# A hybrid attention layer on one core: the framework schedules by its other model of engine times, and the fillers' matmuls are pinned in source order

## The chip, the core and the metric

The kernel runs on one core of a Trainium2 chip. A core has TensorE (PE, matmuls, with its weight loads shown apart as PEld), VectorE (DVE), ScalarE (ACT), GpSimd (POOL) and SyncE (SP, which here issues the DMAs). Each engine works through a program of its own in order, and semaphores make one wait for another. The metric is the time of one execution on the device in microseconds (us).

## The reference

One layer of a hybrid encoder on 1024 positions of width 1024, in float32: a combined input projection, two attention branches of eight heads each with a head dimension of 64, sigmoid gates, an output projection, LayerNorm, a SwiGLU feed-forward part (FFN) and a second LayerNorm.

```python
h = x @ w_in[l]
qa, ka, va, qb, kb, vb, ga, gb = jnp.split(h, split_pts, axis=-1)
y_a = chunk_band_attention(heads_a(qa), heads_a(ka), heads_a(va), rel_bias[l]) @ w_proj_a[l]
y_b = stick_breaking_attention(heads_b(qb), heads_b(kb), heads_b(vb)) @ w_proj_b[l]
gate_a = jax.nn.sigmoid(ga + b_gate[l, :D])
gate_b = jax.nn.sigmoid(gb + b_gate[l, D:])
mix = (gate_a * y_a + gate_b * y_b) @ w_out[l]
x = layer_norm(DEEPNORM_ALPHA * x + mix, ln1_g[l], ln1_b[l])
g, u = jnp.split(x @ w_ffn_in[l], 2, axis=-1)
x = layer_norm(DEEPNORM_ALPHA * x + (jax.nn.silu(g) * u) @ w_ffn_out[l], ln2_g[l], ln2_b[l])
```

Branch A is a softmax over a band of nine chunks of 64 keys with a learned bias. Branch B (stick-breaking) weighs each key by the sigmoid of its score times the product of one minus the sigmoids of the keys between it and the query.

## The kernel before

**Arithmetic.** Every float32 operand of a large product is split into a high and a low part (`split`, L110: a cast on ACT, then a subtraction on DVE), and one product becomes three matmuls, high by high, high by low and low by high. The names end in h and l: wbp1h and wbp1l are the halves of one weight operand of pair 1.

**Stages, in the order of the source.**
- *Projection.* The first pair of weight tiles is multiplied plainly (`project_plain`); each further pair goes through a scheme of seven products for two by two blocks (`pair_steps`, L181). It accumulates in banks of the matmul memory that are named sx, sy and sz, copies them out on ACT and adds them on DVE (L191, tiles c). The operands for it are sums of blocks of x (s13, s24) and of the weights (ta, tb, with wa and wb as their split forms, wc for the last product), which DVE works out (L153 to L157, L277 to L280).
- *Attention.* Heads a0 to a7 of branch A, then b0 to b7 of branch B, each in two groups of four blocks of 128 queries. A block of A (`soft_block`) is: scores on PE (sc_a, L506 and L507), a reduction with bias on DVE (L539), an exponential on ACT, a reciprocal on DVE and a multiplication on POOL (L547). A block of B (`stick_block`) is: scores, two sigmoids on ACT (L572, L573), a running product on DVE (L574) and a product on POOL (L577). Then `value_steps` transposes the weights on PE (tp, L603), splits them (pt) and multiplies them with the values (pv, L617 and L618); a copy on ACT (L627) and an addition on DVE (L631) make the head's result.
- *Fillers.* Between the steps of attention, the generator `fill_all` hands out single matmuls of other work: gate projections (gps, L463) and, from the middle of branch B, the output projection of branch A (yAps, L665).
- *After attention.* The last head pair's result is split into yh7 and yl7, then come the projection of branch B (yBps, matmuls in `mm3`, L118 to L121), the product with w_out (ops), the first LayerNorm, transposes of its result (x1ps, L865), the FFN's up projection in the scheme of seven products (sxf, syf, szf, and plainf for the tile without a partner), its down projection (dn) and the second LayerNorm.

**What sets the order.** The source traces instructions in one order: the loop over the attention's steps runs blocks ahead by the table LEAD, transposes, and takes fillers until the amount given by FILL is used. The framework then schedules: it goes through the program with a model of engine times, and on each engine puts next the first instruction in source order whose inputs are ready by that model. So an instruction traced later can be put ahead of one traced earlier. Tiles share slots and banks in turn (BANKS: two each for mm and sc, three for tr, one for pv), and a new owner waits for the readers of the old one. The result is one fixed list for each engine.

Names in listings below: sc_a3_4_0 is the score bank of head 3 of A, block 4, first part; w_a3_0_2 the weights of head a3, group 0, block 2; tp_a3_0_0 the transposed weights of a group's first pack; the numbers at the end of a name are running numbers of tiles.

## Time and profile before

| | us |
|---|---|
| median of 3 runs | 1448.25 |
| the three runs | 1447.61, 1448.25, 1448.53 |
| the profiled execution's own time | 1447.76 |
| its span in the trace | 1446.0 |

The profile is of one execution. In its rows of groups, "x96 | 100.6, 1057 | 49.5 <-DVE" reads: 96 instructions, 100.6 us in total, 1057 ns each in the mean, 49.5 us of idle time of the engine just ahead of them, most of it ended by DVE. In a timeline each row is the start, the duration, the engine and the line; a value in brackets is the idle time before, and what ended it. PE's matmuls are pipelined, so their durations overlap, and its pace is read from start to start. Line numbers are those of the kernel before; in the changed kernel all lines from 86 on are higher by one.

### The profile page before, as it was taken

Reading aid. Unit: us, or ns where it says so; the run is one execution under the profiler, and the core shown is the slowest. Engines: PE = TensorE matmul, PEld = TensorE weight load, DVE = VectorE, ACT = ScalarE, POOL = GpSimd, SP = SyncE. Lnnn points to the kernel's source line nnn. Section 1 sums busy time; section 2 is a strip of 40 time slices with the busy share of each in tenths; the row PEclk is TensorE's granted clock in tenths of the full one; section 3 lists DMA queues with packets and bytes.
Section 4 is the critical chain, followed back from the end, with each engine's and each line's share of the span. In section 5 each row is a group of like instructions: output and inputs, shape, how many; then the busy total and the mean of one; then the engine's idle time right before and its main releaser. Section 6 shows DMA issues by size and latency. Waiting matters only on the chain.

```text
span 1446.0 us, 18952 instructions
## 1 busy us (share of the span) xinstructions
PE 1411.3 (98%) x6656; PEld 1163.9 (80%) x6656; DVE 1022.1 (71%) x1591; ACT 687.3 (48%) x1204; POOL 313.3 (22%) x339
## 2 busy tenths in 40 slices
PE   7999999999999999999999999999999999999997
PEld 6788888888888788788887878888888788888886
DVE  7867676744888888787769995555565544885996
ACT  6445444435777879784323543333333332444540
POOL 0000000003434769652304021111111101300012
PEclk9999999999999999999999999999999999999999
DMA  6566686748656466757861233233222226863521
GB/s 233 172 216 223 216 266 201 294 155 235 189 166 185 137 192 193 218 171 279 315 234 73 81 138 107 105 109 110 95 90 93 95 102 241 305 210 111 174 80 73
DMA packets 84238, 248.75 MB, mean 172 GB/s; under 512 B 10400, under 2 KB 10400, under 8 KB 84144
## 3 DMA queue, kind: packets, MB, share of 16 engines
q1 hardware_dynamic: 84144, 247.56, 51.7%
q8 instruction: 52, 0.85, 0.3%
q14 instruction: 42, 0.34, 0.1%
HBM read 164.39 MB, written 83.13 MB: 171 GB/s over the span
## 4 chain that ended last, share of the span: by engine, by line
PE 84%; DVE 8%; ACT 3%; DMA 2%; issue 2%; POOL 1%; SPq 0%; POOLq 0%; DVEq 0%; ACTq 0%
PE dn L1145 14%; PE sxf L178 14%; PE sxp L178 12%; PE szf L178 6%; PE szp L178 6%; PE ops L1004 5%; PE gps L463 4%; PE syf L178 4%; PE syp L178 3%; PE yAps L665 2%; PE tp_b L603 2%; PE tp_a L603 1%; PE sc_a L506 1%; DVE kp_b L574 1%; DMA xraw<-in_xt_dram 1%
## 5 line engine op out<-in xcount | busy, mean ns | idle before, releaser
L1145 PE MATMUL dn<-dr,dl 128*128 128x512 f32 x924 | 209.6, 389 | 0.0
L1145 PEld LDWEIGHTS dn<-dr,dl 128*128 128x128 f32 x924 | 173.5, 188 | 36.0
L577 POOL TENSOR_TENSOR w_b<-w_b,kp_b 128x511 f32<-128x511 f32 (+3 forms) x96 | 100.6, 1057 | 49.5 <-DVE kp_b L574 40.2
L574 DVE TENSOR_TENSOR_SCAN kp_b<-kp_b,ident_ps 128x512 f32<-128x512 f32 (+3 forms) x96 | 93.1, 971 | 23.0 <-ACT kp_b L572 17.0
L111 ACT CAST dl<-raw 128x512 fp32r<-128x512 f32 x77 | 47.5, 623 | 84.8 <-PE dn L1145 68.9
L1004 PE MATMUL ops<-wr,wl 128*128 128x512 f32 x336 | 78.8, 392 | 0.0
L841 POOL TENSOR_TENSOR mv<-mv,neghalf 128x1 f32<-128x1 f32 x16 | 25.7, 1609 | 237.0 <-DVE mv L840 237.0
L526 POOL MEMSET bias<- 64x64 f32 x8 | 1.2, 146 | 335.6 <-ACT bias L525 335.5
L1004 PEld LDWEIGHTS ops<-wr,wl 128*128 128x128 f32 x336 | 62.5, 188 | 12.5
L112 DVE TENSOR_TENSOR dl<-raw,dl 128x512 fp32r<-128x512 f32 x77 | 53.5, 702 | 23.7 <-ACT dl L111 23.3
L572 ACT ACTIVATE kp_b<-sc_b 128x512 f32<-128x512 f32 (+3 forms) x96 | 49.5, 516 | 24.8 <-PE sc_b L507 22.8
L547 POOL TENSOR_SCALAR w_a<-w_a,st_a 128x640 f32<-128x640 f32 (+2 forms) x64 | 44.6, 703 | 61.3 <-DVE st_a L546 49.4
L942 POOL TENSOR_TENSOR sb<-h 128x512 f32<-128x512 f32 x10 | 16.8, 1682 | 188.3 <-PE syf L178 102.1
L178 PE MATMUL szf<-x1S63h,wcf 128*128 128x512 f32 x168 | 55.6, 392 | 0.7 <-ACT gt L208 0.6
L112 DVE TENSOR_TENSOR pt_b<-tp_b,pt_b 128x512 fp32r<-128x512 f32 (+1 forms) x80 | 48.4, 621 | 10.8 <-ACT pt_b L111 10.5
L191 DVE TENSOR_TENSOR gt<-sxf,gt 128x512 f32<-128x512 f32 x21 | 14.4, 687 | 55.8 <-PE sxf L178 55.8
L573 ACT ACTIVATE w_b<-sc_b 128x511 f32<-128x511 f32 (+3 forms) x96 | 49.7, 517 | 0.0
L544 ACT ACTIVATE w_a<-w_a,st_a 128x640 f32<-128x640 f32 (+2 forms) x64 | 44.5, 696 | 10.3 <-DVE st_a L539 9.3
L111 ACT CAST pt_b<-tp_b 128x512 fp32r<-128x512 f32 (+1 forms) x80 | 45.4, 576 | 8.0 <-PE tp_b L603 7.5
L603 PE MATMUL tp_b<-ident,w_b 128*128 128x128 f32 x288 | 45.5, 276 | 3.3 <-DVE pt_b L112 3.3
L943 POOL TENSOR_TENSOR sa<-h,h 128x512 f32<-128x512 f32 x10 | 15.9, 1588 | 146.6 <-PE sxf L178 120.1
L112 DVE TENSOR_TENSOR pt_a<-tp_a,pt_a 128x512 fp32r<-128x512 f32 x64 | 41.6, 652 | 6.3 <-ACT pt_a L111 6.0
(1658 smaller groups left out, 4224.2 us busy)
## 6 DMA issues: line engine op xcount, KB each, us to landing
raw<-left_dr SPq DMA_DIRECT2D x77, 256.0 KB, 3.0
wo_dr<-wo SPq DMA_DIRECT2D x28, 512.0 KB, 4.1
wr<-wo_dr SPq DMA_DIRECT2D x28, 512.0 KB, 7.4
wLf<-in_w_ffn_in_dram SPq DMA_DIRECT2D x22, 512.0 KB, 4.5
wRf<-in_w_ffn_in_dram SPq DMA_DIRECT2D x22, 512.0 KB, 4.3
rows<-in_w_ffn_out_dram SPq DMA_DIRECT2D x22, 512.0 KB, 6.3
wLp<-in_w_in_dram SPq DMA_DIRECT2D x17, 512.0 KB, 5.9
wRp<-in_w_in_dram SPq DMA_DIRECT2D x17, 512.0 KB, 5.2
```

What stands on the lines that cost most here:

```text
L111: nc.scalar.copy(dst_h, src)
L112: nc.vector.tensor_tensor(dst_l, src, dst_h.bitcast(F32), ALU.subtract)
L178: mm(acc, lw[:, ks], rx, start=(first and kt == i == 0), stop=(kt == 3 and i == 2), skip_group_check=not first)
L463: mm(acc, lw[:, ks], rx[k][:, cs], start=(k == j == 0), stop=(k == KT - 1 and j == 2))
L547: nc.gpsimd.tensor_scalar(s[:, 0:w], s[:, 0:w], st[:, 3:4], 0.0, ALU.mult, ALU.add)
L572: nc.scalar.activation(kp[:, c0:e], sc[:, 0:n], AF.Sigmoid, scale=-1.0)
L573: nc.scalar.activation(be[:, m0:e], sc[:, m0 - c0:n], AF.Sigmoid)
L574: nc.vector.tensor_tensor_scan(kp[:, c0:e], kp[:, c0:e], ident_ps()[:, 0:n], kp[:, c0 - 1:c0] if c0 else 0.0, ALU.mult, ALU.bypass if c0 e ...
L577: nc.gpsimd.tensor_tensor(be[:, m0:e], be[:, m0:e], kp[:, m0 - 1:e - 1], ALU.mult)
L603: tr(tp[:, j:j + P], wt[qb - q0][:, (kb - qb) * P:(kb - qb + 1) * P], ident)
L1004: mm(acc, lw, rx, start=(fresh and n == m == 0), stop=(n == 3 and m == 2), skip_group_check=not fresh)
L1145: mm(acc, lw, rx, start=(fresh and steps[s][1] == n == 0), stop=(last and n == 2), skip_group_check=not fresh)
```

## The change

Two things. The context in which the program is built gets `schedule_with_timeline_sim=True`: the framework's scheduler takes its times from its other model, a simulation of the engines' timeline, when it asks which instruction is ready. And every matmul of a filler is passed through `tc.keep_in_program_order`, which adds an edge of order without a semaphore to the instruction that was traced before it on the same engine: a filler can no longer be put ahead of that one, while an instruction traced later can still go ahead of a filler.

```diff
+    pin = tc.keep_in_program_order
...
-                    mm(acc, lw[:, ks], rx[k][:, cs], start=(k == j == 0),
-                       stop=(k == KT - 1 and j == 2))
+                    pin(mm(acc, lw[:, ks], rx[k][:, cs], start=(k == j == 0),
+                           stop=(k == KT - 1 and j == 2)))
...
-                            mm(acc, lw[:, ks], rx[k][:, cs], start=(k == n == 0),
-                               stop=(k == 3 and n == 2))
+                            pin(mm(acc, lw[:, ks], rx[k][:, cs], start=(k == n == 0),
+                                   stop=(k == 3 and n == 2)))
...
-    with tile.TileContext(nc) as tc:
+    with tile.TileContext(nc, schedule_with_timeline_sim=True) as tc:
```

The instructions are the same in kind and number on every engine. Their places change: 5107 of PE's 6656 matmuls stand elsewhere in its list (by up to 177 places earlier and 80 later), and so do 1201 instructions of DVE, 812 of ACT, 127 of POOL and 384 DMA issues of SP.

PE at the change from head a3 to a4, before, from the first transposes of a3's first group:

```order
L603 MATMUL tp_a3_0_0_3640<-ident_69,w_a3_0_0_3464 128x128
L603 MATMUL tp_a3_0_0_3640<-ident_69,w_a3_0_1_3492 128x128
L603 MATMUL tp_a3_0_0_3640<-ident_69,w_a3_0_2_3533 128x128
L603 MATMUL tp_a3_0_0_3640<-ident_69,w_a3_0_3_3559 128x128
L463 MATMUL gps11_0_3589<-xh2_295,wh_g11_3000 128x512
L463 MATMUL gps11_0_3589<-xl2_303,wh_g11_3000 128x512
L617 MATMUL pv_a2_1_3629<-pt_a2_1_1_3601,v2_3277 128x384
L618 MATMUL pv_a2_1_3629<-pt_a2_1_1_3601,v2_3277 128x384
L617 MATMUL pv_a2_1_3629<-pt_a2_1_1_3601,v2_3277 128x128
L618 MATMUL pv_a2_1_3629<-pt_a2_1_1_3601,v2_3277 128x128
L463 MATMUL gps11_0_3589<-xh2_295,wl_g11_3001 128x512
L506 MATMUL sc_a3_6_0_3657<-kh3_3308,qs3_3306 128x256
```

and now, from the transpose of the same group's third block:

```order
L604 MATMUL tp_a3_0_2_3699<-ident_69,w_a3_0_2_3533 128x128
L507 MATMUL sc_a3_6_0_3657<-kh3_3308,qs3_3306 128x256
L508 MATMUL sc_a3_6_0_3657<-kl3_3311,qs3_3306 128x256
L507 MATMUL sc_a3_7_0_3665<-kh3_3308,qs3_3306 128x128
L508 MATMUL sc_a3_7_0_3665<-kl3_3311,qs3_3306 128x128
L507 MATMUL sc_a4_0_0_3688<-kh4_3521,qs4_3519 128x320
L508 MATMUL sc_a4_0_0_3688<-kl4_3524,qs4_3519 128x320
L507 MATMUL sc_a4_0_1_3692<-kh4_3521,qs4_3519 128x320
L508 MATMUL sc_a4_0_1_3692<-kl4_3524,qs4_3519 128x320
L604 MATMUL tp_a3_0_0_3640<-ident_69,w_a3_0_3_3559 128x128
L464 MATMUL gps11_0_3589<-xh2_295,wh_g11_3000 128x512
L464 MATMUL gps11_0_3589<-xl2_303,wh_g11_3000 128x512
```

Before, all four transposes of the first pack stood together, with fillers (gps11) and the value products of a2 behind them, and the scores of block 6 after that. Now the scores of blocks 6 and 7 and the first two of head a4 stand ahead of the transpose of the fourth block, and the fillers behind it.

PE at the end of attention, before, from the first matmuls of the projection of branch B up to the first one that uses yh7:

```order
L118 MATMUL yBps2_0_6925<-yh4_6031,wh_yB0_6914 128x512
L119 MATMUL yBps2_0_6925<-yl4_6032,wh_yB0_6914 128x512
L121 MATMUL yBps2_0_6925<-yh4_6031,wl_yB0_6915 128x512
L118 MATMUL yBps2_0_6925<-yh5_6380,wh_yB0_6914 128x512
L119 MATMUL yBps2_0_6925<-yl5_6381,wh_yB0_6914 128x512
L121 MATMUL yBps2_0_6925<-yh5_6380,wl_yB0_6915 128x512
L118 MATMUL yBps2_0_6925<-yh6_6691,wh_yB0_6914 128x512
L119 MATMUL yBps2_0_6925<-yl6_6692,wh_yB0_6914 128x512
L121 MATMUL yBps2_0_6925<-yh6_6691,wl_yB0_6915 128x512
L118 MATMUL yBps2_1_6940<-yh4_6031,wh_yB0_6914 128x512
L119 MATMUL yBps2_1_6940<-yl4_6032,wh_yB0_6914 128x512
L118 MATMUL yBps2_0_6925<-yh7_6908,wh_yB0_6914 128x512
```

and now, from the last value products of head b7:

```order
L619 MATMUL pv_b7_1_6897<-pt_b7_1_1_6875,v15_6537 128x128
L618 MATMUL pv_b7_1_6897<-pt_b7_1_2_6890,v15_6537 128x256
L619 MATMUL pv_b7_1_6897<-pt_b7_1_2_6890,v15_6537 128x256
L119 MATMUL yBps2_0_6925<-yh7_6908,wh_yB0_6914 128x512
L119 MATMUL yBps2_1_6940<-yh7_6908,wh_yB0_6914 128x512
L120 MATMUL yBps2_0_6925<-yl7_6909,wh_yB0_6914 128x512
L122 MATMUL yBps2_0_6925<-yh7_6908,wl_yB0_6915 128x512
L120 MATMUL yBps2_1_6940<-yl7_6909,wh_yB0_6914 128x512
L122 MATMUL yBps2_1_6940<-yh7_6908,wl_yB0_6915 128x512
```

The eleven matmuls on yh4 to yh6 that stood ahead of the first one on yh7 have been moved up, in among the steps of b7; the value products are now followed directly by the matmuls on yh7.

DVE near the start of the projection, where the operands of pair 1 are made, before:

```order
L154 TENSOR_TENSOR tbp1_510<-wRp1_507,tap1_509 128x512
L157 TENSOR_TENSOR tap1_509<-wRp1_507 128x512
L155 TENSOR_TENSOR tbp1_510<-wLp1_333,tbp1_510 128x512
L112 TENSOR_TENSOR wcp1_523<-wRp1_507,wcp1_523 128x512
L326 SCALAR_TENSOR_TENSOR lo0_0_527<-plain0_0_407,hi0_0_526 128x512
L112 TENSOR_TENSOR wbp1l_515<-tbp1_510,wbp1h_514 128x1024
L326 SCALAR_TENSOR_TENSOR lo0_0_527<-plain0_512_457,hi0_0_526 128x512
L112 TENSOR_TENSOR wap1l_520<-tap1_509,wap1h_519 128x1024
L326 SCALAR_TENSOR_TENSOR lo1_0_537<-plain1_0_432,hi1_0_536 128x512
L326 SCALAR_TENSOR_TENSOR lo1_0_537<-plain1_512_482,hi1_0_536 128x512
L191 TENSOR_TENSOR c1_1_559<-syp1_561,c1_1_559 128x512
L191 TENSOR_TENSOR c1_2_588<-syp2_590,c1_2_588 128x512
```

and now:

```order
L192 TENSOR_TENSOR c1_1_559<-syp1_561,c1_1_559 128x512
L154 TENSOR_TENSOR tap1_509<-wRp1_507,wLp1_333 128x512
L158 TENSOR_TENSOR tap1_509<-wRp1_507 128x512
L280 TENSOR_TENSOR s24_3_392<-xraw7_278,s24_3_392 128x512
L155 TENSOR_TENSOR tbp1_510<-wRp1_507,tap1_509 128x512
L192 TENSOR_TENSOR c1_2_588<-syp2_590,c1_2_588 128x512
L156 TENSOR_TENSOR tbp1_510<-wLp1_333,tbp1_510 128x512
L113 TENSOR_TENSOR s24l3_268<-s24_3_392,s24h3_267 128x1024
L113 TENSOR_TENSOR s13l3_270<-s13_3_391,s13h3_269 128x1024
L113 TENSOR_TENSOR wbp1l_515<-tbp1_510,wbp1h_514 128x1024
```

The additions c1_1 and c1_2, which take the banks syp1 and syp2, stood behind the low half wbp1l and now stand ahead of it, as do the splits s24l3 and s13l3, which were made earlier before.

## The prediction

> **What bounds the kernel now.** The page comes first: TensorE (PE) is busy for 98% of the span.

> ```profile
> span 1446.0 us, 18952 instructions
> ...
> PE 1411.3 (98%) x6656; PEld 1163.9 (80%) x6656; DVE 1022.1 (71%) x1591; ACT 687.3 (48%) x1204; POOL 313.3 (22%) x339
> ```

> So 1446.0 - 1411.3 = 34.7 us are all that any order could gain on PE, unless it changes the number of instructions, which this one doesn't. PE's pace is read in the chain of work that ended last:

> ```profile
> 50.36 2.73 PE szp L178 x12
> ```

> 2.73 / 12 = 0.227 us for a 128x512 matmul; narrower ones go by their columns (128 columns: 0.057, an estimate from that row). The list of PE's waits, longest sums first behind the one at the kernel's start, says what the idle time is (us in total, times, longest):

> ```profile
> PE tp_b L603 <- DVE pt_b L112: 3.3, 5, 1.6
> PE pv_b L617 <- ACT yv_b L627: 3.1, 1, 3.1
> PE sxf L178 <- DVE gt L191: 2.7, 4, 1.7
> PE x1ps L865 <- POOL acc L850: 1.8, 1, 1.8
> PE tp_a L603 <- DVE pt_a L112: 1.6, 3, 0.9
> PE sc_a L506 <- DVE st_a L539: 1.6, 2, 1.4
> PE sxp L178 <- ACT c L195: 1.4, 1, 1.4
> ```

> The longest single one among these is at 580 us. PE's timeline and ScalarE's (ACT's) show it, the first number being the start and the second the duration; the windows view then shows the granted clock as the third number from the end, 0.50.

> ```profile
> 580.57 0.40 PE L665 MATMUL yAps<-yh,wh_y 128*128 128x512 f32 x1
> 584.07 0.67 PE L617 MATMUL pv_b<-pt_b,v 128*128 128x512 f32 x1 [3.10 <-ACT yv_b L627]
> ```

> ```profile
> 582.00 1.04 ACT L446 CAST wh_y<-wr_y 128x1024 fp32r<-128x1024 f32 x1 [4.39 <-POOL yl L695]
> ```

> ```profile
> 584.30:587.60 3.30, 3.30 (x11) 2.62 (x11) 3.27 (x4) 2.65 (x6) 0.70 (x1) 0.50 0.72 274
> ```

> ACT works its queue in order. Its cast of wh_y0_3 waited 4.39 us for a GpSimd (POOL) subtraction, everything queued behind stood still, the copy of pv_b's bank among it, and PE stood 3.10 us. Then PE had half its clock for 3.30 us, another 1.65 us. In FFN and down projection no wait of note is left, so attention and the joints between stages decide.

> **The change part by part.** Nothing is added or removed: the terms are waits that come and go, and each is PE's missing cover. I sum against the profiled run's 1447.76 us; the median shown, 1448.25, is 0.49 above it.

> *Attention A, +7.6.* At the change of heads (a1 to a2, a3 to a4, a5 to a6, a7 to b0) the scores of the old head's last blocks and of the new one's first stand one behind the other, with the fillers pinned behind the transposes. Two banks hold scores, so PE waits until VectorE (DVE) has reduced them. DVE's rows from 346 to 470 us, grouped by shape (count | busy, mean ns):

> ```profile
> L539 DVE CUSTOM_DVE_ANT_0 w_a<-sc_a,bias,st_a 128x320 f32<-128x320 f32 x32 | 17.5, 548 | 2.4 <-PE sc_a L507 2.1
> L539 DVE CUSTOM_DVE_ANT_0 w_a<-sc_a,bias 128x320 f32<-128x320 f32 x32 | 15.5, 484 | 2.4 <-PE sc_a L507 2.4
> L546 DVE RECIPROCAL st_a<-st_a 128x1 f32<-128x1 f32 x64 | 10.3, 161 | 7.6 <-ACT w_a L544 6.7
> L539 DVE DVE_READ_ACCUMULATOR2_ANT st_a<- 128x1 f32 x96 | 7.9, 83 | 0.0
> L631 DVE TENSOR_TENSOR yt<-yt 64x1024 f32<-64x1024 f32 x4 | 6.3, 1568 | 0.2
> ...
> L539 DVE CUSTOM_DVE_ANT_0 w_a<-sc_a,bias 128x512 f32<-128x512 f32 x8 | 5.5, 690 | 0.4 <-PE sc_a L507 0.4
> ```

> Behind the last score of a3's fourth block DVE has 548 + 83, the head's addition of 1568, 690 + 83 for 512 columns, some 560 + 83 for 384 and 420 + 83 for 256 (both read between the rows by columns), two reciprocals of 161 and 280 + 83 for 128: 4.8 us before sc_a4_0_1 finds a bank. PE has there, by columns, 0.11 of pv, 8 score matmuls of 1.13, one pair of 320 at 0.28 and five transposes at 0.11 each: 2.1. The stall is 2.7. It is at least 1.1, if the addition of 1.57 is done beforehand, and 3.0, if it waits some 0.3 for its copy; a gain is excluded, since DVE's queue is in order. Four changes: 4 x 2.7 = 10.8 (4.4 to 12.0). Against that go the waits tp_a 1.6 and sc_a 1.6, whose places all move; I credit them whole, and keep nothing as the other end. 10.8 - 3.2 = +7.6. Inside a head the weights take this long to come, from the first row's start to the last one's end (scores, then POOL's second multiplication):

> ```profile
> 395.33 0.31 PE L507 MATMUL sc_a<-kl,qs 128*128 128x320 f32 x1
> ...
> 397.01 1.58 POOL L547 TENSOR_SCALAR w_a<-w_a,st_a 128x640 f32<-128x640 f32 x2 [0.46 <-DVE st_a L546]
> ```

> That is 398.59 - 395.64 = 2.95 behind the score. By the new order PE has 1.8 to 4.2 us of work there, 2.5 to 4.1 before: a short head loses up to 1.1, a long one nothing; at the head changes this hides in the stall above, so no term.

> *Attention B, -1.3.* The block at 580 goes: ACT now has 12 operations between the cast of yh4 and that of wh_y0_3, with two before, by which time POOL is through. Credit: 3.1 + 1.65, and tp_b's 3.3, together 8.1. New is the shorter cover between the fourth block's last score and the first transpose of its weights: before, 4.0 us of PE work in b0 and 6.0 in the others; now 3.5, 2.5, 2.5, 3.6, 2.5, 4.2, 2.5, 1.8 for b0 to b7, counted in the order at pace. What it must cover, at b3:

> ```profile
> 543.94 0.31 PE L507 MATMUL sc_b<-kl,qs 128*128 128x320 f32 x1
> ```

> ```profile
> 544.43 2.92 POOL L577 TENSOR_TENSOR w_b<-w_b,kp_b 128x448 f32<-128x448 f32 x3 [0.37 <-DVE kp_b L574]
> ```

> From the score's end to POOL's third product 547.35 - 544.25 = 3.1. With this the shortfalls are 0.6 four times and 1.3 at b7: 3.7. With one more POOL product ahead (2.92 / 3 = 0.97) they are 9.8. Below nothing is excluded, since these waits are in PE's own queue; of 3.7 and 9.8 I take the middle, 6.8, as no row is nearer to either: 6.8 - 8.1 = -1.3. If the block should not go, the term is +3.5.

> *End of attention, +3.3.* The fillers are used earlier, so nothing lies between the last pv_b7 and the first matmul on yh7:

> ```profile
> 668.70 0.28 PE L618 MATMUL pv_b<-pt_b,v 128*128 128x256 f32 x1
> ...
> 671.67 0.50 PE L118 MATMUL yBps<-yh,wh_yB 128*128 128x512 f32 x1 [0.19 <-ACT yh L111]
> ```

> ```profile
> 671.65 1.23 DVE L112 TENSOR_TENSOR yl<-yt,yh 128x1024 fp32r<-128x1024 f32 x1 [1.12 <-ACT yh L111]
> ```

> The chain from 668.70 (plus 0.11 for 256 columns) to 671.67 took 2.85 us: copy, addition, cast. Before, 11 matmuls (2.5) covered it but for some 0.35; now none do: +2.5. Then two matmuls (0.45) stand ahead of the first on yl7, which comes at 672.88: 672.88 - 671.67 - 0.45 = 0.8. The 11 matmuls are in the cover counted for b7. Low 2.5, high 3.6 (the same with DVE busy with another 0.3); below nothing isn't possible, as the chain is fixed.

> *Start of the projection, +1.6.*

> ```profile
> 43.35 0.39 PE L178 MATMUL syp<-xh,wlp2l 128*128 128x512 f32 x1
> 45.16 0.50 PE L178 MATMUL sxp<-s24h,wbp1h 128*128 128x512 f32 x1 [1.42 <-ACT c L195]
> ```

> ```profile
> 44.66 1.22 DVE L112 TENSOR_TENSOR wbp1l<-tbp,wbp1h 128x1024 fp32r<-128x1024 f32 x1
> ...
> 48.73 1.28 DVE L191 TENSOR_TENSOR c<-syp,c 128x512 f32<-128x512 f32 x2
> ```

> Before, wbp1l ended at 45.88, just when PE asked for it. Now three more lo operations and two additions c stand ahead of it and one wcp behind: four more at 0.60 (1.28 for two, overlapped), 2.4 us. Two szp matmuls (0.45) are pulled into the gap, and the 1.42 that PE waited before overlaps part of the delay; wap1l comes later in turn. I take +1.6, between 0 (all of it beside PE's earlier work) and 2.4 + 0.6.

> *Bank reuse in the projection, +1.5.* At three later pairs 2 matmuls (0.45) instead of 12 (2.72) stand between the last read of an sxp bank and its next write, and DVE's addition (0.6 by the last row) comes between: at least 0.2 each, at most 0.6 + 1.22 - 0.45 = 1.4 with a split ahead of it (row of wbp1l). By the nearer end, 0.5 each.

> *Behind LN1, +2.9.* plainf0_512 now follows the last transpose group x1ps1_7 directly and needs the bank that Silu frees:

> ```profile
> 812.20 0.59 ACT L111 CAST x1A<-x1ps 128x512 fp32r<-128x512 f32 x1 [0.75 <-PE x1ps L865]
> 812.81 1.28 ACT L931 ACT_TABLE_LOAD   x1
> 814.11 0.60 ACT L931 ACTIVATE gt<-plainf 128x512 f32<-128x512 f32 x1
> ```

> 0.59 + 1.28 + 0.60 plus hand-over is 2.7; the three x1ps groups now one behind the other wait some 2.0 for their banks (three casts of 0.59); the 1.8 for POOL goes. 2.7 + 2.0 - 1.8 = 2.9 (0.2 if the table is loaded early, 4.0 if the additions queue).

> *FFN, DMA, SP's and POOL's queues, 0.* 384 of SP's issues change places, but the waits list above has no DMA in it; between a weight's issue and its first matmul in the FFN stand 54 us of PE work, 57 before, and 69 for 65. Cover gone would show as PE waits there, at the sxf waits of 2.7 first: bounds -2.7 to +2.7.

> Sum: 7.6 - 1.3 + 3.3 + 1.6 + 1.5 + 2.9 = +15.6: 1447.76 + 15.6 = 1463.4, **1463**.

> *The clock.* The 3.10 us wait was followed by 0.50; a new wait of 2.7 may be or may not. [...]

> **The rivals.**
> 1. *The new waits also halve the clock.* Six are 2.7 or more (four head changes, the end, plainf0_512), near the 3.10 that did; the wait of 1.42 did not visibly. Each costs 1.65: 9.9, so 1473.
> 2. *Faster: covers hold in attention.* With fillers pinned tight the weights are ready when their transposes come, as DVE meets its reductions early. Its place are the heads' changes; for it speaks that DVE is idle for 29% of the span, against it that the 4.8 us there are serial. A: -3.2 (no new stall), B: -8.1, end +3.3, start 0, banks +0.5, LN1 +0.2: -7.3, 1440.5. It decides from where ten new waits (four in A, six in B) cost less than (7.3 - 2.9) / 10 = 0.44 each, against 1.8 each taken here.
> 3. *Waits come and go in equal parts.* PE's 34.7 idle us only move, if the head changes cost 1.1 each (-6.4), B's cover 3.7 (-3.1), the start nothing (-1.6) and LN1 0.2 (-2.7): 15.6 - 13.8 = +1.8, 1449.6. Each of these is a low end, and all four must come together.
> 4. *The change does nothing.* Excluded: 5107 of PE's 6656 matmuls stand at another place.

> **How the numbers follow.** Forecast 1452 to 1474, 0.60: around 1463 with A at 4.4 (-6.4) and LN1 at 0.2 (-2.7) together with FFN's -2.7, 1451.6, up to the highs of A, B, start and banks, 1.2 + 3.0 + 1.4 + 2.7 = 8.3, with FFN's +2.7, 1474.4. Rival 1: 0.15, rival 2: 0.15, rival 3: 0.10. A measurement of this kernel tells some 0.2% (2.9 us) from no change. Faster 0.15, same 0.10, slower 0.75. The range of 1442 to 1478 leaves out most of rival 2 and the upper part of rival 1.

> **What would show it.** In the trace after: PE waits for st_a at sc_a of four head changes, 2 to 3 us each; no POOL wait of wh_y0_3 on ACT and no 0.50 clock near 580 us; a wait of 2.5 or more at the first yBps on yh7; plainf waiting for gt; wbp1l ending near 48. It would be wrong if sc_a waits sum to less than 4 us, if tp_b's stay at 3.3, or if an FFN wait for a DMA appears.

## The result and the profile after

| | us |
|---|---|
| changed kernel, median of 4 runs | 1502.16 (1499.59 to 1505.84) |
| before, median of 4 runs beside them | 1447.96 (1447.61 to 1448.53) |
| ratio, 95% interval | 1.0377 (1.0362 to 1.0391) |
| profiled execution after, its span | 1499.59, 1497.8 |

The forecast was 1463 with a range up to 1478: the direction was right, and the size was off by a factor of more than three. The page of the changed kernel, to be held against that of before:

```profile
span 1497.8 us, 18996 instructions
...
PE 1430.9 (96%) x6656; PEld 1180.8 (79%) x6656; DVE 1025.5 (68%) x1591; ACT 689.8 (46%) x1204; POOL 324.7 (22%) x339
```

PE's matmuls are the same 6656, and the span is 51.8 us longer, but PE's busy time has risen too, by 19.6 us. A busy time that rises for the same matmuls says that they ran slower. Both parts show in the list of PE's waits (total, times, longest) and in the windows.

```profile
PE sxp L179 <- ACT c L196: 12.1, 5, 3.9
PE sc_a L507 <- DVE st_a L540: 11.0, 11, 3.3
PE tp_b L604 <- DVE pt_b L113: 6.5, 7, 1.6
...
PE sxp L179 <- ACT wbp1h L112: 3.5, 1, 3.5
PE dn L1146 <- ACT dl L112: 2.9, 1, 2.9
PE yBps L119 <- ACT yh L112: 2.7, 1, 2.7
PE plainf L931 <- ACT gt L932: 2.6, 1, 2.6
```

The windows view of before, for projection, branch A and branch B (each stage up to the start of the next one's first score or of the last pv_b7; the third number from the end is the granted clock):

```profile
0.00:349.00 349.00, 339.03 (x1504) 276.19 (x1505) 228.17 (x315) 160.88 (x238) 4.00 (x14) 1.00 0.67 219
349.00:466.70 117.70, 115.50 (x711) 99.06 (x710) 95.83 (x317) 90.75 (x212) 51.42 (x78) 1.00 0.64 188
466.70:668.70 202.00, 193.25 (x1068) 162.65 (x1066) 166.52 (x218) 158.97 (x334) 133.33 (x171) 0.99 0.60 185
```

and of the changed kernel:

```profile
0.00:366.20 366.20, 341.88 (x1468) 277.27 (x1469) 228.33 (x313) 156.72 (x235) 1.30 (x11) 0.97 0.59 202
366.20:509.30 143.10, 129.56 (x738) 110.24 (x738) 96.16 (x318) 94.24 (x211) 50.78 (x79) 0.94 0.59 174
509.30:719.10 209.80, 199.41 (x1093) 167.04 (x1093) 164.68 (x219) 160.32 (x337) 133.18 (x174) 0.99 0.56 175
```

The projection runs at 0.97 of the clock and branch A at 0.94, where both ran at 1.00.

A stage's length alone misleads, since 36 matmuls have moved from the projection's stretch to behind it. So I worked out the excess: for each PE instruction, the time to the start of the next one less its pace (0.227 us for 512 columns, in proportion for fewer, 0.109 for a transpose), summed by stage up to the end of the down projection; and, as a bound on what the clock took of it, the time at half the granted clock, halved.

| stage | excess before | after | difference | forecast | by the clock, at most: before | after |
|---|---|---|---|---|---|---|
| projection | 9.5 | 35.0 | +25.5 | +3.1 | 0 | 12.0 |
| attention A | 13.2 | 31.9 | +18.7 | +7.6 | 0 | 8.5 |
| attention B | 20.5 | 22.8 | +2.3 | -1.3 | 1.7 | 1.7 |
| end of attention, w_out | 1.1 | 5.0 | +3.9 | +3.3 | 0 | 1.7 |
| LN1, FFN up | 10.0 | 8.4 | -1.6 | +2.9 | 0 | 3.4 |
| down projection | 0.0 | 3.1 | +3.1 | 0 | 0 | 0 |
| sum | 54.3 | 106.3 | +52.0 | +15.6 | 1.7 | 27.3 |

The sum accounts for the span's 51.8 us. At most half of it, 25.6, is clock. That is a bound, since in part of the half-clock time PE stood anyway; the rise of PE's busy time, 19.6 us, is nearer to what the slower matmuls took. The rest is waits.

**Where the waits come from.** The largest in the projection is at pair 4. SP's queue, ACT's and PE's, at 108 to 117 us of the changed kernel:

```profile
108.71 1.87 SPq L306 DMA_DIRECT2D q_dr<-hi  x2
```

```profile
115.49 0.58 ACT L196 COPY c<-sxp 128x512 f32<-128x512 f32 x1 [8.04 <-DMA q_dr<-hi]
```

```profile
111.88 0.39 PE L179 MATMUL szp<-s24h,wcp 128*128 128x512 f32 x1
116.12 0.80 PE L179 MATMUL sxp<-s24h,wbp4h 128*128 128x512 f32 x1 [3.86 <-ACT c L196]
116.72 0.63 PE L179 MATMUL sxp<-s24l,wbp4h 128*128 128x512 f32 x1
```

ACT's copy c1_4 has its operand, but the slot of its output still holds hi1_3, which is being stored: its two issues begin at 108.71, and the copy starts only at 115.49, 6.8 us later. PE may not add into the bank sxp4 before it is copied, and waits 3.86 us; then the next matmul is 0.60 behind and the following ones 0.43 where 0.23 is the pace. In the kernel before the same store was issued at 97.46 and 99.53, and the copy came at 103.67, 6.2 us behind the first of them, with no wait in front of it:

```profile
97.46 0.88 SPq L305 DMA_DIRECT2D q_dr<-hi  x1
...
99.53 0.83 SPq L305 DMA_DIRECT2D q_dr<-hi  x1
```

```profile
103.67 0.59 ACT L195 COPY c<-sxp 128x512 f32<-128x512 f32 x1
```

There PE asked for the bank only at 107.82:

```profile
107.82 0.39 PE L178 MATMUL sxp<-s24h,wbp4h 128*128 128x512 f32 x1
```

That is 3.6 us behind the copy's end at 104.26. Between pair 3's last product and this matmul PE had 57 matmuls (12.9 us at pace); in the new order it has 36 (8.2 us). So 4.8 us of cover are gone; the store's first issue comes 5.0 us behind the start of that last product, where it came 2.9 behind it; and from issue to copy it takes 0.6 longer. 4.8 + 2.1 + 0.6 - 3.6 = 3.9, the wait that PE has. The same happens at pairs 7 and 10.

The largest wait in branch A is at 438 us, in the head change a3 to a4. From SP, ACT, DVE and PE:

```profile
428.10 0.34 SPq L446 DMA_DIRECT2D wr_g<-in_w_in_dram  x1
```

```profile
435.80 1.04 ACT L447 CAST wh_g<-wr_g 128x1024 fp32r<-128x1024 f32 x1 [3.90 <-DMA wr_g<-in_w_in_dram]
```

```profile
437.70 0.16 DVE L547 RECIPROCAL st_a<-st_a 128x1 f32<-128x1 f32 x1 [4.46 <-ACT w_a L545]
```

```profile
438.43 0.44 PE L507 MATMUL sc_a<-kh,qs 128*128 128x384 f32 x1 [3.34 <-DVE st_a L540]
```

ACT's list has the cast of the filler weight wh_g14 so early that its load, issued at 428.10, comes 7.6 us later. ACT stands 3.90 us, the exponentials behind it stand with it, DVE waits 4.46 for one of them, and PE 3.34 for DVE. The first matmul on wh_g14 starts at 551 us. Before, 65 PE instructions lay between the load's issue and this cast, now 24, and the cast waited for nothing:

```profile
405.31 1.06 ACT L446 CAST wh_g<-wr_g 128x1024 fp32r<-128x1024 f32 x1
```

ACT's list of waits for DMAs says the same of the whole. Before:

```profile
ACT wh_g L446 <- DMA wr_g<-in_w_in_dram: 4.8, 2, 2.5
```

and after:

```profile
ACT wh_g L447 <- DMA wr_g<-in_w_in_dram: 19.2, 6, 4.1
ACT c L196 <- DMA q_dr<-hi: 15.9, 2, 8.0
ACT c L209 <- DMA k_dr<-hi: 14.1, 3, 5.0
ACT dl L112 <- DMA raw<-left_dr: 14.0, 12, 4.3
...
ACT gB L701 <- DMA gB<-g_dr: 10.4, 6, 6.8
```

In the list of before these sums were 4.8 for wh_g, 1.0 for c and q_dr, none for c and k_dr, 8.8 for dl and 1.0 for gB.

### The profile page after: what moved, and what is told of

Its sections match the earlier page's. It is cut to its first block, busy times and chain, and to the rows that moved or that the text cites. A ratio compares the mean times of both kernels' runs of the same rounds, so it can differ in the third digit from the quotient of the medians.

```text
span 1497.8 us, 18996 instructions
## 1 busy us (share of the span) xinstructions
PE 1430.9 (96%) x6656; PEld 1180.8 (79%) x6656; DVE 1025.5 (68%) x1591; ACT 689.8 (46%) x1204; POOL 324.7 (22%) x339
## 4 chain that ended last, share of the span: by engine, by line
PE 83%; DMA 6%; DVE 5%; ACT 3%; issue 2%; POOL 1%; SPq 1%; POOLq 0%; DVEq 0%; ACTq 0%
PE sxf L179 15%; PE dn L1146 12%; PE sxp L179 9%; PE szf L179 7%; PE ops L1005 5%; PE gps L464 4%; PE szp L179 4%; PE syf L179 4%; PE syp L179 3%; PE yAps L666 2%; PE tp_b L604 2%; PE tp_a L604 2%; PE plainf L931 2%; DMA v_dr<-v 1%; PE yBps L119 1%
## 5 line engine op out<-in xcount | busy, mean ns | idle before, releaser
L112 ACT CAST dl<-raw 128x512 fp32r<-128x512 f32 x77 | 47.7, 623 | 80.4 <-PE dn L1146 63.5
L113 DVE TENSOR_TENSOR dl<-raw,dl 128x512 fp32r<-128x512 f32 x77 | 52.7, 686 | 30.6 <-ACT dl L112 30.4
L1005 PEld LDWEIGHTS ops<-wr,wl 128*128 128x128 f32 x336 | 62.7, 188 | 12.9
L943 POOL TENSOR_TENSOR sb<-h 128x512 f32<-128x512 f32 x10 | 18.2, 1818 | 213.0 <-DVE h L987 153.4
L113 DVE TENSOR_TENSOR pt_b<-tp_b,pt_b 128x512 fp32r<-128x512 f32 (+1 forms) x80 | 48.5, 623 | 18.2 <-ACT pt_b L112 18.0
L573 ACT ACTIVATE kp_b<-sc_b 128x512 f32<-128x512 f32 (+3 forms) x96 | 49.0, 510 | 21.1 <-PE sc_b L508 14.5
L112 ACT CAST pt_b<-tp_b 128x512 fp32r<-128x512 f32 (+1 forms) x80 | 45.0, 574 | 16.4 <-PE tp_b L604 16.1
L574 ACT ACTIVATE w_b<-sc_b 128x511 f32<-128x511 f32 (+3 forms) x96 | 49.2, 513 | 0.0
L604 PEld LDWEIGHTS tp_b<-ident,w_b 128*128 128x128 f32 x288 | 35.4, 140 | 16.8 <-DVE pt_b L113 7.3
L113 DVE TENSOR_TENSOR dr<-rows,dr 128x512 fp32r<-128x512 f32 x66 | 44.7, 684 | 2.2 <-ACT dr L112 2.1
L507 PE MATMUL sc_a<-kh,qs 128*128 128x320 f32 (+2 forms) x96 | 35.1, 368 | 11.7 <-DVE st_a L540 11.0
```

What stands on the lines that cost most here:

```text
L112: nc.scalar.copy(dst_h, src)
L113: nc.vector.tensor_tensor(dst_l, src, dst_h.bitcast(F32), ALU.subtract)
L573: nc.scalar.activation(kp[:, c0:e], sc[:, 0:n], AF.Sigmoid, scale=-1.0)
L574: nc.scalar.activation(be[:, m0:e], sc[:, m0 - c0:n], AF.Sigmoid)
L604: tr(tp[:, j:j + P], wt[qb - q0][:, (kb - qb) * P:(kb - qb + 1) * P], ident)
L1005: mm(acc, lw, rx, start=(fresh and n == m == 0), stop=(n == 3 and m == 2), skip_group_check=not fresh)
```

## The experiments

Theory 1 is that the new model places work on ACT (and with it PE's) as if DMAs landed sooner than they do. Its rival is the prediction's own: the serial queue of DVE and short covers on PE. What the model assumes inside no run shows; theory 1 speaks of the lists that it made. In all tables "excess" is the number defined above.

**e1 and e2: each half of the change alone.**

```diff
e1   -    with tile.TileContext(nc) as tc:
e1   +    with tile.TileContext(nc, schedule_with_timeline_sim=True) as tc:
...
e2   +                    pin(mm(acc, lw[:, ks], rx[k][:, cs], start=(k == j == 0),
e2   +                           stop=(k == KT - 1 and j == 2)))
```

> The other model alone, without the pins. The order of the first 1468 of PE's matmuls is word for word that of the changed kernel. Theory 1 (the model makes the new order, and the projection's loss is its own): the projection loses the same 25.6 us against before as in the changed kernel (first sc_a0 at 366 us), and since the fillers are now drawn forward into the first heads of A and are missing later, the whole is slower than the changed kernel, 1505 to 1550 us. Theory 2 (the model and the pins are harmful only together, because the pins hold the fillers behind late transposes): A's 18.7 us go for the most part, 1478 to 1490 us.

> The pins alone, with the scheduler's old model. 186 of PE's 6656 matmuls change places, all at the change from projection to attention and in the first heads of A, none of SP's issues. Theory 1 (the model carries the loss): 1444 to 1452 us, no difference that can be told. Theory 2 (the pins carry a part): fillers held behind late transposes cost in A at least 5 us, 1453 us or more.

Measured: e1 1524.06 us, ratio 1.0517 (1.0493 to 1.0541); e2 1450.43, ratio 1.0018 (1.0009 to 1.0027). The model carries the loss: e1's projection has an excess of 33.9, as the changed kernel's 35.0. Without the pins B is worse by 30.6 us (53.4 against 22.8): the fillers are used up early, and PE has 916 matmuls in B where it has 1093 in the changed kernel. So the pins help this model; beside the old one they cost A 3.5 us of excess. From the list of PE's waits of e1:

```profile
PE sxp L178 <- ACT c L195: 12.8, 5, 4.3
PE tp_b L603 <- DVE pt_b L112: 12.3, 15, 1.8
```

**e3, e6 and e7: attention's PE order undone.** Scores, transposes and value products are pinned in source order; e7 does this with the old model, as a control, and e6 adds the pins of e5.

```diff
-        mm(sc[:, 0:n], q, hd["kh"][:, ksl], start=True, stop=False)
+        pin(mm(sc[:, 0:n], q, hd["kh"][:, ksl], start=True, stop=False))
...
-                        tr(tp[:, j:j + P], wt[qb - q0][:, (kb - qb) * P:(kb - qb + 1) * P], ident)
+                        pin(tr(tp[:, j:j + P], wt[qb - q0][:, (kb - qb) * P:(kb - qb + 1) * P], ident))
...
-                    mm(pv[0][:, cs], v[:, kb, :], pt[:, o:o + n], start=(i == m == 0), stop=False)
+                    pin(mm(pv[0][:, cs], v[:, kb, :], pt[:, o:o + n], start=(i == m == 0), stop=False))
```

> The changed kernel with the scores, the transposes and the value products of attention pinned too: PE's order in attention is then the source's, in branch B word for word that of the kernel before; projection, LN1 and FFN keep the changed kernel's order, but for 192 matmuls after attention. Theory 1 (each stage's loss is its own): A's 18.7 us and B's 2.3 go, all but 1 to 3 us; the projection's 25.6 stay: 1479 to 1486 us. Theory 2 (the order on DVE, ACT and SP carries A's loss, since they are not pinned): less than 8 us go, above 1494 us.

> The kernel before (old model) with fillers, scores, transposes and value products pinned: a control for e3. Theory 1 (the source's order of PE in attention is harmless by itself but for the first head, whose scores no longer lie among the projection's last matmuls): 1450 to 1457 us. Theory 2 (pinning PE there costs by itself what e3 lost): 1465 us or more.

> The kernel of e3 (attention's PE order pinned) with the casts and gate sigmoids of e5 pinned as well. Theory 1 (what was left of A's loss in e3 is ACT standing for wr_g13 and wr_g14): the waits of 3.9 at tp_a and of 3.3 at pv_a go, with the half clock behind them: A's excess falls from 29.9 by 8 to 14 us, 1488 to 1497 us. Theory 2 (the order on DVE and ACT as such): the same as e3 within 4 us.

Measured: e3 1507.1 us (ratio 1.0401), e7 1458.88 (1.0074), e6 1487.01 (one run). e3 missed what I expected of theory 1 by 20 us: A's excess is 29.9, hardly less than 31.9. Its control says half of why: the source's order costs A 12.8 us by itself (26.0 in e7 against 13.2), also a miss, between the two theories. The other half is e6: with the casts pinned as well A's excess is 20.0, 10 less than e3 and 6 less than the control. So casts that wait for their loads make a good part of A's loss, whatever PE's order is. What the new order of PE itself cost in A e3 can't say, since the source's order isn't that of the kernel before; e10 takes that up.

**e4: another slot for c1.**

```diff
+                if side == "1" and i in (4, 7, 10):
+                    turn_of[QK] += 1
                 tl[side] = cycle(QK, f"c{side}_{i}")
```

> The changed kernel, in which the tiles c1 of pairs 4, 7 and 10 take the next slot of their cycle: they then wait for the store of wo5 instead of the store of hi1 of the pair before, which is the last thing that pair does. Theory 1 (PE waits at sxp4, sxp7 and sxp10 for this slot, 3.9, 3.7 and 3.3 us, and then runs at half clock for 3.4 + 1.7 + 3.4 us lost): the three waits go and the clock stays at 1.0 behind them: 10.9 + 8.5 = 19 us less, 1480 to 1488 us. Theory 2 (the order is too tight there anyhow, so another slot or bank is late next): less than 8 us less, above 1494 us.

Measured: 1480.31 us, ratio 1.0216 (1.0191 to 1.024). The windows view from 95 to 270 us, of the changed kernel and of e4:

```profile
95.00:270.00 175.00, 162.19 (x693) 131.04 (x692) 103.27 (x141) 71.55 (x109) 0.00 (x0) 0.95 0.59 203
```

```profile
95.00:270.00 175.00, 171.91 (x776) 140.68 (x775) 118.24 (x161) 79.06 (x123) 0.00 (x0) 1.00 0.65 225
```

In the same 175 us PE does 776 matmuls and not 693, at a clock of 1.00 and not 0.95. The projection's excess falls from 35.0 to 15.2: up to 10.3 of that 19.8 by the clock (12.0 to 1.7), the rest waits. That the wait went through the slot is shown by the rows above, store, copy and PE. e4 doesn't part the slot from the order: freed of the slot, the scheduler made another list, in which some 500 of the projection's 1468 matmuls stand elsewhere and the first product that needs c1_4 stands ahead of pair 3's last one.

**e5 and e8: the casts pinned.**

```diff
-        nc.scalar.copy(hi, r)
+        pin(nc.scalar.copy(hi, r))
...
-        nc.scalar.activation(t, t, AF.Sigmoid, bias=bg[:, col:col + 1])
+        pin(nc.scalar.activation(t, t, AF.Sigmoid, bias=bg[:, col:col + 1]))
```

> The changed kernel with two ACT operations pinned behind the ACT instruction traced before them: the cast of a filler weight (wh_g, wh_y, wh_yB) and the sigmoid of a reloaded gate (gA, gB). The cast of wh_g14 then stands behind the copy gate12 and not 24 PE instructions behind its load. Theory 1 (the model places ACT's work on loaded tiles before the loads have landed, and ACT's queue stands for it): ACT's waits for wr_g (19.2 us) fall below 8; the stalls in A whose chain ends in wr_g12, wr_g13 and wr_g14 (0.7 + 2.5 + 3.5 + 1.0 = 7.7) and the two half clocks behind them (3.4 each) go, up to 14.5 us: 1487 to 1492 us. Theory 2 (DVE's serial queue at the change of heads makes A's loss, as the prediction had it): less than 5 us go, above 1497 us.

> The edits of e4 and of e5 together in the changed kernel. Theory 1 (both losses come from queues that stand for DMAs, at places apart): the gains add, e4's 20 us (measured 1480) and e5's: 1464 to 1472 us. Theory 2 (what one frees the other takes): 1476 us or more.

Measured: e5 1488.28 us (ratio 1.0270, 1.0249 to 1.0291), e8 1466.2 (1.0117, 1.0099 to 1.0134). Both as theory 1 had it, and the gains add: 13.9 for e5, 21.9 for e4, 36.0 for both. ACT's waits for wr_g are gone from e5's list. The longest wait for st_a in e5 is 1.2 us, where it was 3.3:

```profile
PE sc_a L507 <- DVE st_a L540: 7.0, 11, 1.2
```

A's excess falls from 31.9 to 25.5 in e5, and B's from 22.8 to 18.2. In A PE's list stays the same but for some 60 matmuls; in B some 600 stand elsewhere, so that B's gain can't be put down to the casts alone.

**e10: DVE's part in the head changes.** e8 without the addition of a head's halves in branch A; y_a is then not the reference's.

```diff
-                    elif g == 1:
+                    elif g == 1 and hd["br"]:
                         nc.vector.tensor_tensor(yt[r], both[0:DH], both[DH:P], ALU.add)
```

> The kernel of e8 without DVE's addition of the two halves of a head's result in branch A (8 operations of 1.2 to 1.6 us), so that y_a isn't the reference's. Theory 1 (at the four head changes of A PE waits for DVE's serial queue, of which the addition is the longest piece, 1.35, 1.34, 1.35 and 1.18 us in e8): these four waits fall to 0.3 or less, with the half clock of 1.7 to 3.4 us behind one or two of them: 4 to 8 us less than e8, 1458 to 1462 us. Theory 2 (PE waits for the two score banks as such, whatever DVE does between): less than 2 us less, 1464 us or more.

What it takes away, in e8's timeline of DVE and PE at the change a3 to a4:

```profile
410.76 1.22 DVE L634 TENSOR_TENSOR yt<-yt 64x1024 f32<-64x1024 f32 x1 [0.40 <-ACT yt L630]
411.90 0.68 DVE L542 CUSTOM_DVE_ANT_0 w_a<-sc_a,bias 128x512 f32<-128x512 f32 x1
```

```profile
412.64 0.39 PE L509 MATMUL sc_a<-kh,qs 128*128 128x256 f32 x1 [1.17 <-DVE st_a L542]
```

The addition, then the reduction of the next block, then PE has a bank. Measured: 1462.69 us against e8's 1466.2; A's excess falls from 23.6 to 16.9, 3.4 of it by the clock. The total is a little above what I expected, and by itself proves little, as the ratios' intervals overlap (1.0080 to 1.0126 here, 1.0099 to 1.0134 in e8). The traces do: PE's list in A is the same in both, and the waits at the four changes, 1.2 to 1.4 us each in e8, are gone from PE's timeline. So the prediction's mechanism was there.

**e13 and e14: PE kept busy in the waits.** 15 or 8 matmuls without use are pinned into the waits at sxp4, sxp7 and sxp10.

```diff
+            if nm in ("p4", "p7", "p10"):
+                warm = bank("pv", f"warm{nm}")
+                for n in range(15):
+                    pin(mm(warm, W["hl"][0][:, 0:P], xh[n % 8][:, LO], start=True, stop=True))
```

> The changed kernel with 15 added matmuls (3.4 us at pace) of no use, into a bank that nothing reads, pinned into each of PE's three long waits at sxp4, sxp7 and sxp10 (3.9, 3.7 and 3.3 us); the waits for the slot stay. Theory 1 (the half clock comes from PE's idleness in the wait and is a cost of its own): the granted clock stays at 1.0 behind the three, 3.4 + 1.7 + 3.4 = 8.5 us less than the changed kernel, 1491 to 1496 us. Theory 2 (the slow matmuls behind a wait have another cause, so that busy PE changes nothing): 1500 us or more.

> As e13 with 8 added matmuls (1.8 us) in each wait, so that some 2.1, 1.9 and 1.5 us of idle time are left in one piece. Theory 1 (a wait halves the clock only when it is long, 2.7 us or more, as the prediction had it): clock 1.0 behind all three, the same as e13. Theory 2 (shorter waits do it too, if they fall so): half the clock behind one to three of them, 1.7 us each, 2 to 5 us above e13.

The windows view behind the wait at sxp4, of the changed kernel and of e13:

```profile
116.20:119.50 3.30, 3.30 (x8) 2.63 (x9) 0.59 (x1) 0.00 (x0) 0.00 (x0) 0.50 0.00 0
```

```profile
116.20:119.50 3.30, 3.30 (x15) 2.72 (x16) 3.02 (x4) 0.41 (x1) 0.00 (x0) 1.00 0.00 0
```

In the same 3.3 us PE runs 15 matmuls and not 8. Behind all three waits, where the changed kernel has 0.50, the clock is 1.00 in e13, with PE kept busy there. In e14 a wait of 1.76 us is left there, also with the clock at 1.00 behind it:

```profile
115.94 0.50 PE L179 MATMUL sxp<-s24h,wbp4h 128*128 128x512 f32 x1 [1.76 <-ACT c L196]
```

In e14 the clock fell behind the third of the three only, where 2.11 us of wait were left (1.7 us lost at 244 to 252). So half the clock came behind a wait well below 2.7 us, as theory 2 had it. The total misses what was expected: e13 1505.51 us (1496.29 to 1508.25), e14 1497.16 (1496.81 to 1509.83). Branch A begins at 361.6 in e13, 4.6 us sooner than in the changed kernel and not 8.5; waits at the slots of other pairs and at kh0's load have grown, and the later stages' excess differs by several us from run to run. On the total these two say nothing that their spread would bear.

**e9, e11 and e12: the same pin in the kernel before.** e9 pins all casts of load_w with the old model, e11 the gates' sigmoids too, e12 only the fillers' casts. The edit of e12:

```diff
-        nc.scalar.copy(hi, r)
+        cast = nc.scalar.copy(hi, r)
+        if not name.startswith("yB"):
+            pin(cast)
```

> The kernel before (old model, no pinned filler) with only the casts of the filler weights pinned behind the ACT instruction traced before them. Theory 1 (ACT's queue stands in the kernel before too, at 577.6 us for 4.39 us, and PE pays 3.1 us and 1.7 us of clock): that block goes, 1442 to 1446 us, faster than before by 0.2 to 0.4%. Theory 2 (the casts that now come later are late next for their matmuls or for POOL's low halves): 1447 us or more.

> As e9, with the sigmoids of the reloaded gates pinned too, as in e5. Theory 1: the same as e9 within 2 us, 1441 to 1447 us, since ACT stands for no gate in the kernel before. Theory 2 (a gate's sigmoid pinned late holds the bank of yAps, so PE waits for mm banks): 3 us or more above e9.

> The kernel of e9 without the pin on the casts of wh_yB, the weights of branch B's projection, so that only the filler weights' casts (wh_g, wh_y) are pinned in the kernel before. Theory 1 (e9 lost at wh_yB0 behind yh7, 3.4 us and the clock behind it, what the block at 580 us had given): 5 to 6 us less than e9, 1443 to 1446 us, at or a little below the kernel before. Theory 2 (e9's loss is in the heads): 1448 us or more.

Measured: e9 1450.52 us (ratio 1.0012, 1.0003 to 1.0020), e11 1450.88 (1.0015), both misses; e12 1446.94 against 1447.94 beside it, ratio 0.9990 (0.9981 to 0.9999). PE's waits in e9:

```profile
PE tp_b L604 <- DVE pt_b L113: 5.1, 4, 2.2
PE yBps L119 <- ACT wh_yB L447: 3.4, 1, 3.4
```

The block at 580 us is gone, but the cast of wh_yB0 is now pinned behind yh7, and PE waits 3.4 us for it. e12 takes that back, and gains the 0.1% that its interval allows: the waits for pt_b's low half, 3.3 before, are 6.1 in it, with half the clock behind the longest of 2.2 us (0.81 and 0.76 in the mean of 516 to 520 and 520 to 524 us), so most of what the block gave is given back in B. It is the fastest of the kernels here, by less than 0.2%.

## Why the prediction was wrong

The step that failed is "FFN, DMA, SP's and POOL's queues, 0". It argued that the list of waits of before has no DMA in it, and priced 384 moved DMA issues, and all the ACT work on what they load or store, at nothing. That list shows which cover holds in the old order; it says nothing of how little is left over. At c1_4 3.6 us were left, and the new order took 21 matmuls, 4.8 us, of cover. I had counted distances for the FFN's weights only. And the list was PE's: ACT's own list of before has waits for DMAs (8.8 us for dl, 4.8 for wh_g), so it could be seen there that ACT's queue stands for them. The waits of ACT above for stores (slots) and for filler weights are what the term left out: of the changed kernel's waits on PE, those whose chain I could follow back to a DMA sum to 27.6 us of excess, 12.9 at the slots of five pairs, 7.7 at filler weights, 2.5 at kh0 and kl0, 1.5 at a gate and 3.0 in the down projection:

```profile
1306.47 0.62 ACT L112 CAST dl<-raw 128x512 fp32r<-128x512 f32 x1 [4.25 <-DMA raw<-left_dr]
```

The second is the clock. Rival 1 had it, with a chance of 0.15 and a price of 9.9 us for six waits; it took some 20 to 25.6.

By the terms:

- *Attention A, +7.6, was +18.7.* The mechanism was right (e10) and over-sized: a wait of 1.2 to 1.4 us and one of 0.4 behind it at a1 and a5, not 2.7. What made up the rest was ACT's queue at a0 and a3, 7.7 us, and up to 8.5 of clock.
- *Attention B, -1.3, was +2.3.* The block at 580 went, as was said. The cover was not the limit that I took it for: of the new waits most are for pt_b's low half on DVE, where the products kp and the head's addition stand ahead (6.5 us, with 3.3 before).
- *End of attention, +3.3, was +3.9.* The wait of 2.7 us for yh7 is the one foreseen; the 0.8 for yl7 hid behind matmuls at half clock, which took up to 1.7 in its place:

```profile
722.10 0.79 PE L119 MATMUL yBps<-yh,wh_yB 128*128 128x512 f32 x1 [2.69 <-ACT yh L112]
```

- *Start of the projection, +1.6:* the waits grew as foreseen, from 2.5 to 4.1 us, but for another operand and with up to 3.4 of clock behind them. I followed wbp1l on DVE; PE waited for wbp1h, which stands behind two casts on ACT that had to wait for DVE themselves:

```profile
45.99 0.58 PE L179 MATMUL sxp<-s24h,wbp1h 128*128 128x512 f32 x1 [3.49 <-ACT wbp1h L112]
```

```profile
43.00 1.04 ACT L112 CAST s24h<-s 128x1024 fp32r<-128x1024 f32 x1 [2.59 <-DVE s L280]
43.95 1.04 ACT L112 CAST s13h<-s 128x1024 fp32r<-128x1024 f32 x1
44.89 1.04 ACT L112 CAST wbp1h<-tbp 128x1024 fp32r<-128x1024 f32 x1
```

- *Bank reuse, +1.5:* the three waits for DVE's addition sum to 1.0. Right; the larger ones were at other pairs, for ACT's copy.
- *Behind LN1, +2.9:* the waits at x1ps and plainf rose from 1.8 to 4.7 us, as foreseen, and up to 3.4 of clock came with them. Against that the excess ahead of sxf and szf fell from 6.5 to 0.2, of which the list of waits of before shows 3.3 (sxf 2.7, szf 0.6); my bound of -2.7 was too narrow. The sum is -1.6.

```profile
871.86 0.79 PE L931 MATMUL plainf<-x1A,wlf0h 128*128 128x512 f32 x1 [2.58 <-ACT gt L932]
```

- *The clock:* the prediction left open whether a new wait of 2.7 us halves it, and its sum held nothing for that. In the changed kernel half the clock came behind shorter waits too, of 1.35 and 1.39 us at a5 and a7; up to PE's last matmul each stretch of half clock was 3.4 or 6.8 us long.

Of the three signs of being wrong, the first did not come: the waits of sc_a for st_a sum to 11.0 us. The other two did: tp_b's waits rose from 3.3 to 6.5, and a wait for a DMA appeared in the down projection.

Not settled: e8 is still 18 us of excess over the kernel before, 10.4 in A (e10 finds 6.7 of them at the head changes), 5.1 at the end of attention, 3.5 in the projection and 2.8 in the down projection, with 2.7 and 1.3 won in B and the FFN. At the end part of it is the price of the pin itself, as in e9:

```profile
PE yBps L119 <- ACT wh_yB L449: 3.4, 1, 3.4
```

The start and the down projection were not tried apart, nor was e12's exception for wh_yB in this kernel.

## What to carry to other kernels

Before an engine's list is reordered, count for each DMA, loads and stores alike, how much work lies between its issue and the first instruction that needs the tile or its slot, and compare that with the time that the trace shows from issue to start (6 to 8 us here); a wait that isn't there before tells nothing of the margin. An instruction that needs a DMA and isn't urgent holds up what stands behind it in its queue (ACT stood 3.90 us at the cast of wh_g14 here), so place it by when its result is used. On PE, price a new wait with its length and 1.7 to 3.4 us for half the clock behind it, as lost here; that came behind some waits and not behind others (behind 1.8 us in e14's down projection, not behind 2.9 in the changed kernel's).

## What the runs showed of the hardware

```profile
1304.40:1307.80 3.40, 3.40 (x10) 2.63 (x9) 3.40 (x6) 1.11 (x3) 0.00 (x0) 0.50 1.05 403
```

```profile
1307.20:1310.60 3.40, 3.40 (x15) 2.83 (x16) 3.12 (x6) 2.27 (x4) 0.00 (x0) 1.00 1.04 392
```

- With useless matmuls in the three waits at sxp4, sxp7 and sxp10 the clock behind them stayed at 1.00 (e13), where it was 0.50 in the changed kernel.
- The changed kernel and its variants scatter more than the kernel before, and why is not shown: the changed kernel's four runs lie 6.3 us apart and e14's 13.0, the 23 runs of the kernel before beside e9 5.9, but e5's four only 3.2.
